# Sample queries times cached keys, and probabilities times cached values: fp32 on quarters of the array in place of split operands on the whole

## The chip, the core and the metric

The kernel runs on one core of a Trainium2 chip. A core has a matmul engine (PE, with its weight loads shown apart as PEld), three engines for elementwise work (DVE, ACT, POOL), a queue engine that issues transfers (SP), and 16 DMA engines. The metric is the device time of one launch in microseconds; less is better. PE's clock can be granted at one of two levels, 1.2 or 2.4 GHz; the profile shows the share of the full clock.

## What is computed

One decoder layer serves 512 prompt tokens and 64 sample tokens (eight sequences of eight) with shared weights, in three sub-layers: a block of token mixers, cross-attention into a memory of 256 tokens, and a squared-ReLU MLP. The change is in the cross-attention of the sample tokens, where each sequence has its own cached keys and values:

```python
def cross_attn(h, mem_k, mem_v, w_xq, w_xo):
    B, L, _ = h.shape
    q = (h @ w_xq).reshape(B, L, XA_HEADS, XA_DH)                 # 4 heads of 256
    s = jnp.einsum('blhd,bmhd->bhlm', q, mem_k) * (XA_DH ** -0.5) # 256 memory tokens
    p = jax.nn.softmax(s, axis=-1)
    o = jnp.einsum('bhlm,bmhd->blhd', p, mem_v).reshape(B, L, D_MODEL)
    return o @ w_xo
```

All inputs are fp32. For the sample that is 8 sequences x (256 keys and 256 values) x 1024 features, 16 MB of cached data that are read once.

## The kernel before

**Products.** The kernel keeps fp32 accuracy with a faster type of PE, fp32r: each operand is split into a rounded part (hi) and the rest (lo), and a product is three matmuls, hi x hi, lo x hi, hi x lo (`mm3`, lines 190 to 192). Splitting takes a cast on ACT (L90) and a subtraction on DVE (L91).

**Halves.** The 576 tokens are worked on in two halves of 288: 256 prompt and 32 sample tokens (four sequences) each. `project` (line 367 on) multiplies a half with a 1024 x 1024 weight matrix, in eight pieces of 512 KB; one piece is 24 matmuls of 288 columns into `psg` ("a block of 24" below). For the second half the last two pieces of the first are still there.

**The stream of pieces.** Weights, cached keys and cached values come as pieces [128, 1024] in one fixed order (`plan`), through four raw buffers (`wraw`). `wnext` hands out the next split piece and sees to it that two are split and up to three more are on their way; `wfetch` issues the transfer on SP, `wsplit` casts and subtracts. A raw buffer is free again once its piece is split. `KV_AFTER` says how many of the 8 key and 8 value pieces of a half are used after each of the eight weight pieces of a projection: those of half 0 among the pieces of w_xq (for half 1 of the tokens), those of half 1 among the pieces of w_xo (for half 0). In the same gaps a stage of the prompt's attention runs (`tick`).

**Sample attention.** `keys(half)` and `values(half)` in `cross` give a step for each piece. A key piece holds, for one sequence, two heads in two parts of 128 features. For it `pad` (lines 1053 to 1061) clears an operand `qx` [128, 4, 128] and copies hi and lo of the eight queries into their own columns, so that all sequences, pairs of heads, and hi and lo add up in one accumulator `pso` [128 rows, 2 x 256]; then eight matmuls of 256 columns run (L1086). After the eighth piece `merge` adds the rows of hi and lo (`ssum`, L1045 and L1046), a softmax follows (L965 to L973), transposes (L1069), and for each value piece again a padded, split operand (`pad_p`, L1093 to L1099) and eight matmuls (L1126). The result is merged and transposed (L1110) and split into the output projection's operand.

**What sets the order.** Each engine runs its instructions in the order that the build gives them; what a wait holds up is all that stands behind it on its engine. Key pieces of a half are called K0 to K7 below and value pieces V0 to V7; a run is a row of such pieces with no other work between.

Of the kernel before, what the change touches and what calls it, by code (L numbers as in the profile page):

```python
# [22 lines left out]
# order of the mixers: (head, retention)  # L23
UNITS = ((0, 1), (0, 0), (1, 0), (1, 1), (2, 0), (2, 1), (3, 0), (3, 1))
# [8 lines left out]
# columns of the packed constants  # L33
# [21 lines left out]
def decoder_step(ctx, tc, xT, memT, ktc, vc, s_gla, s_ret, w_in, w_ga, w_a2, w_mix, w_xq, w_xk, w_xv, w_xo,  # L55
# [24 lines left out]
    # until the first operands arrive: the table of the activations, and the array's clock  # L80
# [58 lines left out]
    # for the second half of the tokens, the last two pieces are still there, and the first few if kept  # L139
    def keep(ts, n):  # L140
        return ts[:2] + [(t, True) for t in ts[2:2 + n]] + ts[2 + n:]
# [9 lines left out]
    def kvtiles(a, half):  # L151
        return [flat(a[half * 4 + b])[:, m * 1024:(m + 1) * 1024] for b in range(4) for m in range(2)]
# [11 lines left out]
    def wfetch():  # L164
        if plan:
            src = plan.pop(0)
            src, stay = src if isinstance(src, tuple) else (src, False)
            raw = wp.tile([P, 1024], F32, name="wraw", bufs=4)
            nc.sync.dma_start(out=raw if len(src.shape) == 2 else raw.rearrange("p (k n) -> p k n", n=src.shape[2]), in_=src)
            raws.append((raw, stay))  # L170
# [23 lines left out]
    def gemm(ps, w, xh, xl, c, k0=0, k1=KT):  # L194
        """ps = w.T @ x for columns c, over k-tiles."""
# [13 lines left out]
    def meansq(ss, n, t, eps=EPS):  # L209
        """mean + eps, tokens on partitions [t, n], from partial sums of squares [128, any, n*t]."""  # L210
# [25 lines left out]
    def bcast(dg, n, t):  # L236
        """the same on all partitions [128, n*t] (PSUM)"""
# [4 lines left out]
    def sumsq(ss, src, first, eng=nc.vector):  # L242
        """ss += src**2, with src [128, 2, n]."""
# [8 lines left out]
    def prenorm(src, half, g, oh, ol, ss):  # L252
        """(oh, ol) = split of rmsnorm(src) on one half of the tokens."""
# [147 lines left out]
    def to(y, g, ss):  # L401
        """y = g * result, ss = partial sums of the result squared"""
# [9 lines left out]
    def residual(y, r, half, ss, ss2=None, g2=None, oh=None, ol=None, scale=None, done=None):  # L412
        """res = r(pair) + norm(y), y with its gain; (oh, ol) = split of g2 * res, ss2 = partial sums of res**2"""
# [22 lines left out]
    kk = biga.tile([P, 2, 2, 1024], F32R, name="kk", tag="biga")        # [d, hi/lo, pair of heads, (h dt m)]  # L436
    vv = kvp.tile([P, 2, 2, 1024], F32R, name="vv")                     # [m, hi/lo, mt, (h d)]
# [808 lines left out]
```

## Time and profile before

| | |
|---|---|
| three runs | 1235.25, 1236.43, 1236.87 us (median 1236.43) |
| span of the profiled execution | 1236.8 us |
| PE busy | 1208.1 us, 98% |
| DVE, ACT, POOL busy | 60%, 46%, 15% |
| DMA | 149.5 MB, 121 GB/s in the mean |
| matmuls for sample keys (L1086) and values (L1126) | 128 each, 256 columns |
| pieces of cached keys and values | 32, 512 KB each |

The profile is of one execution of the program. A row of the timeline gives the start of an instruction and how long it lasted; matmuls are pipelined, so a matmul starts long before the one ahead has ended, and the cost of one is the distance between two starts. "x2" in a row are two records in one row. `a<-b,c` means that tile a is written from b and c; "128\*128" in a matmul's row is the part of the array that it uses, rows by columns, and then come rows and columns of the moving operand.

### The profile page before, as it was taken

How to read it: one execution, taken by the hardware profiler on the slowest of the kernel's cores; microseconds unless marked ns; L12 is line 12 of the kernel's file. 1: busy time of each engine (PE TensorE's matmuls, PEld its weight loads, DVE VectorE, ACT ScalarE, POOL GpSimd, SP SyncE). 2: the span in 40 equal slices, each digit the busy share in tenths (PEclk: the TensorE clock that was granted, in tenths of full speed). 3: DMA queues.
4: the chain of work that ended last, by engine and by line, in shares of the span. 5: the costliest groups of instructions: out<-in, count | busy, mean ns of one | idle time of the engine just before them, and what ended most of it. 6: DMA issues, size and time to landing. Idle time of an engine off the chain costs nothing.

```text
span 1236.8 us, 22417 instructions
## 1 busy us (share of the span) xinstructions
PE 1208.1 (98%) x9202; PEld 1195.9 (97%) x9202; DVE 737.7 (60%) x1287; ACT 567.4 (46%) x1016; POOL 179.3 (15%) x208
## 2 busy tenths in 40 slices
PE   8999999999999999999999999999999999999995
PEld 8999999999999999999999998999999999999995
DVE  6757666666756675668677777793124334323544
ACT  6624555534553455445666667663223213212431
POOL 1521213131312131210013131000000000000000
PEclk9999999999999999999999999999999999999998
DMA  8753324233323242424555566342222222222402
GB/s 269 245 178 100 122 86 124 86 108 100 112 87 122 86 124 86 124 83 139 183 172 166 191 216 212 120 154 68 86 86 86 84 76 80 86 86 86 137 7 71
DMA packets 60374, 149.46 MB, mean 121 GB/s; under 512 B 5520, under 2 KB 30224, under 8 KB 60144
## 3 DMA queue, kind: packets, MB, share of 16 engines
q1 hardware_dynamic: 60272, 148.04, 38.3%
q8 instruction: 72, 1.18, 0.4%
q14 instruction: 30, 0.25, 0.1%
HBM read 134.12 MB, written 13.89 MB: 120 GB/s over the span
## 4 chain that ended last, share of the span: by engine, by line
PE 90%; DVE 3%; ACT 2%; DMA 2%; POOL 1%; issue 1%; POOLq 0%; SPq 0%; DVEq 0%; ACTq 0%
PE psg L190 26%; PE psg L192 26%; PE psg L191 26%; DVE wl L91 1%; PE psa L190 1%; PE psa L192 1%; PE psa L191 1%; ACT wh L90 1%; PE psa L215 1%; DMA wraw<-in_w_xq 1%; PE pso L1086 1%; PE psa L765 1%; PE pso L891 1%; PE pso L892 1%; PE psa L893 1%
## 5 line engine op out<-in xcount | busy, mean ns | idle before, releaser
L190 PE MATMUL psg<-xh,wh 128*128 128x288 f32 x1808 | 536.1, 297 | 1.2 <-DVE y L567 0.6
L191 PE MATMUL psg<-xh,wl 128*128 128x288 f32 x1808 | 532.5, 295 | 1.7 <-DVE wl L91 1.7
L192 PE MATMUL psg<-xl,wh 128*128 128x288 f32 x1808 | 532.5, 295 | 0.0
L190 PEld LDWEIGHTS psg<-xh,wh 128*128 128x128 f32 x1808 | 339.3, 188 | 2.6 <-issue 1.0
L191 PEld LDWEIGHTS psg<-xh,wl 128*128 128x128 f32 x1808 | 339.3, 188 | 2.3 <-DVE wl L91 2.1
L192 PEld LDWEIGHTS psg<-xl,wh 128*128 128x128 f32 x1808 | 338.8, 188 | 1.0 <-DVE xl L91 0.8
L91 DVE TENSOR_TENSOR wl<-wraw,wh 128x1024 fp32r<-128x1024 f32 x221 | 271.4, 1232 | 94.3 <-ACT wh L90 93.5
L90 ACT CAST wh<-wraw 128x1024 fp32r<-128x1024 f32 x221 | 230.7, 1049 | 169.6 <-PE psg L192 130.0
L190 PE MATMUL psg<-bh,wh 128*128 128x288 f32 x640 | 189.4, 296 | 1.1 <-DMA xr<-in_xT 1.1
L192 PE MATMUL psg<-bl,wh 128*128 128x288 f32 x640 | 188.7, 295 | 0.0
L191 PE MATMUL psg<-bh,wl 128*128 128x288 f32 x640 | 188.6, 295 | 0.0
L190 PEld LDWEIGHTS psg<-bh,wh 128*128 128x128 f32 x640 | 120.1, 188 | 1.8 <-ACT wh L90 1.3
L191 PEld LDWEIGHTS psg<-bh,wl 128*128 128x128 f32 x640 | 120.1, 188 | 0.3 <-DVE wl L91 0.2
L192 PEld LDWEIGHTS psg<-bl,wh 128*128 128x128 f32 x640 | 120.0, 188 | 0.2 <-DVE bl L91 0.2
L228 POOL TENSOR_TENSOR rs<-ms,mhalf 96x3 f32<-96x3 f32 (+1 forms) x9 | 8.8, 983 | 522.3 <-DVE ms L227 408.5
L530 DVE TENSOR_TENSOR hr<-hr 128x576 f32<-128x576 f32 x32 | 24.2, 757 | 90.4 <-ACT hr L529 90.4
L529 ACT ACTIVATE hr<-psg 128x576 f32<-128x576 f32 x32 | 20.8, 651 | 106.7 <-PE psg L192 106.7
L549 DVE TENSOR_TENSOR y<-psg,y 128x576 f32<-128x576 f32 x16 | 12.1, 757 | 62.7 <-PE psg L192 62.7
L751 ACT COPY vt<-psg 128x512 f32<-128x512 f32 x16 | 9.4, 586 | 77.8 <-PE psg L192 77.8
L680 POOL TENSOR_TENSOR rs<-mv,mhalf 128x1 f32<-128x1 f32 (+1 forms) x40 | 26.8, 670 | 108.4 <-DVE mv L675 60.7
L753 DVE COPY vd<-psg 128x96 f32<-128x96 f32 x32 | 6.7, 251 | 50.7 <-ACT vt L751 50.7
L869 POOL TENSOR_TENSOR ks<-kx,ks 32x512 fp32r<-32x512 f32 x16 | 22.6, 1411 | 96.8 <-ACT ks L868 85.6
(284 smaller groups left out, 1745.0 us busy)
## 6 DMA issues: line engine op xcount, KB each, us to landing
wraw<-in_w_in SPq DMA_DIRECT2D x64, 512.0 KB, 3.7
wraw<-in_w_up SPq DMA_DIRECT2D x34, 512.0 KB, 3.6
wraw<-in_w_down SPq DMA_DIRECT2D x34, 512.0 KB, 3.6
wraw<-in_ktc SPq DMA_DIRECT2D x16, 512.0 KB, 4.6
wraw<-in_vc SPq DMA_DIRECT2D x16, 512.0 KB, 4.5
wraw<-in_w_xq SPq DMA_DIRECT2D x14, 512.0 KB, 4.0
wraw<-in_w_xo SPq DMA_DIRECT2D x14, 512.0 KB, 4.5
wraw<-in_w_mix SPq DMA_DIRECT2D x12, 512.0 KB, 5.0
```

Of the source, the lines that this page charges most:

```text
L90: nc.scalar.copy(hi, src)
L91: nc.vector.tensor_tensor(out=lo, in0=src, in1=f32(hi), op=ALU.subtract)
L190: nc.tensor.matmul(out, ah, bh, start=first, stop=False)
L191: nc.tensor.matmul(out, al, bh, start=False, stop=False)
L192: nc.tensor.matmul(out, ah, bl, start=False, stop=last)
L215: nc.tensor.matmul(ps[:t, i:i + 1], ss[:, l, i * t:(i + 1) * t], ones[:, 0:1], start=l == 0, stop=l == ls - 1)
L529: nc.scalar.activation(r, ps, AF.Relu)
L530: nc.vector.tensor_tensor(out=r, in0=r, in1=r, op=ALU.mult)
L680: nc.gpsimd.tensor_tensor(out=rs[:t], in0=mv[:t], in1=mhalf[:t, 0:1], op=ALU.pow)
L765: nc.tensor.matmul(sc[:, :P], kf[:, ci], qf[:, ci], start=True, stop=True)
L869: nc.gpsimd.tensor_tensor(out=ks[32:64], in0=kx[32:64], in1=f32(ks[32:64]), op=ALU.subtract)
L891: nc.tensor.matmul(so[:, :256], lq, s0h[:, j], start=False, stop=False)
```

## The change

- Cached keys and values are no longer split. `wsplit` passes a raw piece on as it is (mode RAW), and its products read the raw buffer. It is free again when these have run. The four raw buffers stay four; a raw piece that waits to be used counts among the three that may be on their way.
- The operands of the sample are fp32 and made once per half: `operand()` clears [128, 8, 4, 32], four sums of hi and lo put the queries in. For the values, four copies out of the transposed probabilities do the same.
- Four matmuls per piece in place of eight, one for each head: 32 columns of the stationary operand (four sequences of eight), on the head's own 32 columns of the array (`tile_position=(0, 32 * h)`), and so into 32 rows of the accumulator. The cached keys are laid out so that a piece holds all four heads of one part.
- With a row for each head and token there is nothing to merge: the softmax runs on [128, 1, 256] straight from the accumulator, and there are two transposes of 128 x 128 where there were four of 64 x 64.
- `KV_AFTER` spreads the pieces as 2, 3, 3, 0, 3, 3, 2, 0 over the weight pieces, before 4, 4, 0, 3, 3, 2, 0, 0.

```diff
-KV_AFTER = (((0, 4), (4, 8), (8, 8), (8, 11), (11, 14), (14, 16), (16, 16), (16, 16)),
-            ((0, 4), (4, 8), (8, 8), (8, 11), (11, 14), (14, 16), (16, 16), (16, 16)))
+KV_AFTER = (((0, 2), (2, 5), (5, 8), (8, 8), (8, 11), (11, 14), (14, 16), (16, 16)),) * 2
...
     def kvtiles(a, half):
-        return [flat(a[half * 4 + b])[:, m * 1024:(m + 1) * 1024] for b in range(4) for m in range(2)]
+        return [(flat(a[half * 4 + b])[:, m * 1024:(m + 1) * 1024], RAW) for b in range(4) for m in range(2)]
...
     def wsplit():
         if raws:
-            raw, stay = raws.pop(0)
-            pool = staying[-1] if stay else wp
+            raw, mode = raws.pop(0)
+            if mode == RAW:
+                ready.append((raw,))
+                return
+            pool = staying[-1] if mode == STAY else wp
...
     def wnext(n=P):
-        while len(ready) < 2 and (raws or plan):
-            while len(raws) < 3 and plan:
+        while sum(len(r) == 2 for r in ready) < 2 and (raws or plan):
+            while plan and len(raws) + sum(len(r) == 1 for r in ready) < N_RAW - 1:
                 wfetch()
+            if not raws:
+                break
             wsplit()
...
+    def operand():
+        x = x1.tile([P, KT, 4, 32], F32, name="qx")
+        nc.gpsimd.memset(x, 0.0)
+        return x
+
+    def quarters(acc, x, w, first, last):
+        for h in range(HEADS):
+            rows = slice(32 * h, 32 * h + 32)
+            nc.tensor.matmul(acc[rows, :256], x(h), w[:, h], start=first, stop=last, skip_group_check=True,
+                             tile_position=(0, 32 * h))
...
     def keys(half):
         c0 = half * NH + 256
         s = Env({"i": 0, "acc": None})
-
-        def pad(b, m):
...
+        qx = operand()
+        for b in range(4):
             qc = slice(c0 + b * 8, c0 + b * 8 + 8)
...
+            nc.gpsimd.tensor_tensor(out=qx[:, :, b, b * 8:b * 8 + 8], in0=f32(qh[:, :, qc]), in1=f32(ql[:, :, qc]), op=ALU.add)
...
         def step():
...
-            for n in range(4):
-                out = s.acc[:, (n // 2) * 256:(n // 2 + 1) * 256]
-                for kx in w:
-                    nc.tensor.matmul(out, q[:, n, :], kx[:, n], start=s.i == 1 and n == 0 and kx is w[0],
-                                     stop=s.i == 8 and n == 3 and kx is w[1], skip_group_check=True)
+            w, = wnext(256)
+            quarters(s.acc, lambda h: qx[:, 2 * h + dt, b], w, s.i == 1, s.i == 8)
             if s.i == 8:
-                pend[half] = softmax(merge(s.acc), 64, "psm", rsx[half][:64, 2:3])
+                pend[half] = softmax(s.acc[:, :256].rearrange("p (j m) -> p j m", j=1), P, "psm", rsx[half][:, 2:3])
                 e.side.append(turn())
```

How the instructions stand, at three places. First PE, where K0 of the first half ends, before (`pso` is the accumulator, `wh` and `wl` the split piece, `psg` the projection, `kk` the prompt's keys, `bh` and `bl` its queries; the numbers tell buffers apart):

```order
L1086 MATMUL pso_8447<-wh_8384,qx_8448 128x256
L1086 MATMUL pso_8447<-wl_8385,qx_8448 128x256
L190 MATMUL psa_8488<-kk_7494,bh_8090 128x256
L191 MATMUL psa_8488<-kk_7494,bl_8091 128x256
L1086 MATMUL pso_8447<-wh_8454,qx_8458 128x256
L192 MATMUL psa_8488<-kk_7494,bh_8090 128x256
L190 MATMUL psa_8488<-kk_7494,bh_8090 128x256
L191 MATMUL psa_8488<-kk_7494,bl_8091 128x256
```

PE at the start of the same piece after (x4 are the four heads of one piece; `wraw` is the raw piece):

```order
L199 MATMUL psg_8424<-xh_7489,wl_8310 128x288
L200 MATMUL psg_8424<-xl_7490,wh_8309 128x288
L1056 MATMUL pso_8449<-wraw_8307,qx_8418 32x256 x4
L1056 MATMUL pso_8449<-wraw_8341,qx_8418 32x256 x4
L198 MATMUL psa_8460<-kk_7494,bh_8090 128x256
L199 MATMUL psa_8460<-kk_7494,bl_8091 128x256
L200 MATMUL psa_8460<-kk_7494,bh_8090 128x256
L198 MATMUL psa_8460<-kk_7494,bh_8090 128x256
```

The eight matmuls of a piece, hi and lo in turn on the whole array, became four on 32 columns each; K0 and K1 stand as one run, and the prompt's products are no longer mixed into them. In each half the quarters stand in nine runs: K0 K1, K2 K3, K4, K5 K6, K7, V0 V1, V2, V3 V4 V5, V6 V7.

Second DVE, from the last key product of the first half to the scaled probabilities `psm`, before (in brackets what an instruction waits for; `xl` belongs to the prompt's attention, `p` and `smx` to both softmaxes):

```order
L1046 TENSOR_TENSOR ssum<-pso,ssum 32x512 [waits Activation_49]
L965 TENSOR_REDUCE mx<-ssum 64x2 [waits DVE_49]
L965 TENSOR_REDUCE mx<-psa 128x2 [waits PE_49]
L966 TENSOR_SCALAR mx<-mx,rsx_82 64x2 [waits DVE_49]
L966 TENSOR_SCALAR mx<-mx,rsx_82 128x2 [waits DVE_49]
L91 TENSOR_TENSOR xl<-psa,xh 128x2x256 [waits Activation_49]
L91 TENSOR_TENSOR wl<-wraw,wh 128x1024 [waits DMAHW4_49]
L971 RECIPROCAL smx<-smx 64x2 [waits Activation_49]
L973 TENSOR_SCALAR psm<-psm,smx 64x256 [waits DVE_49]
L973 TENSOR_SCALAR psm<-psm,smx 64x256
```

The same stretch of DVE after:

```order
L93 TENSOR_TENSOR wl<-wraw,wh 128x1024 [waits DMAHW2_49,Activation_49]
L973 TENSOR_REDUCE mx<-pso 128x1 [waits PE_49]
L93 TENSOR_TENSOR xl<-psa,xh 128x2x256 [waits Activation_49]
L974 TENSOR_SCALAR mx<-mx,rsx_82 128x1 [waits DVE_49]
L93 TENSOR_TENSOR wl<-wraw,wh 128x1024 [waits DMAHW3_49,Activation_49]
L980 RECIPROCAL smx<-smx 128x1 [waits Activation_49]
L93 TENSOR_TENSOR xl<-psa,xh 128x2x256 [waits Activation_49]
L982 TENSOR_SCALAR psm<-psm,smx 128x256 [waits DVE_49]
```

The second merge and half the columns are gone, the maximum comes from the accumulator, and between it and `psm` stand two `xl` and one `wl`.

Third SP, eight transfers from V3 of the first half on, before (DVE is the split that frees the buffer):

```order
L169 DMA wraw_8853<-in_vc 128x1024 [waits DMAHW3_49,DVE_49,Activation_49]
L169 DMA wraw_8897<-in_vc 128x1024 [waits DMAHW4_49,DVE_49,Activation_49]
L169 DMA wraw_8925<-in_vc 128x1024 [waits DMAHW5_49,DVE_49]
L169 DMA wraw_8955<-in_w_xq 128x1024 [waits DMAHW6_49,DVE_49,Activation_49]
L169 DMA wraw_8975<-in_vc 128x1024 [waits DMAHW7_49,DVE_49,Activation_49]
L169 DMA wraw_9010<-in_vc 128x1024 [waits DMAHW0_49,DVE_49]
L169 DMA wraw_9045<-in_w_xq 128x1024 [waits DMAHW1_49,DVE_49]
L169 DMA wraw_9077<-in_w_xq 128x1024 [waits DMAHW2_49,DVE_49,Activation_49]
```

SP from V3 on after (PE is the product that frees the buffer):

```order
L172 DMA wraw_8800<-in_vc 128x1024 [waits DMAHW4_49,PE_49]
L172 DMA wraw_8821<-in_vc 128x1024 [waits DMAHW7_49,DVE_49]
L172 DMA wraw_8842<-in_vc 128x1024 [waits DMAHW5_49,PE_49]
L172 DMA wraw_8874<-in_w_xq 128x1024 [waits DMAHW6_49,PE_49]
L172 DMA wraw_8880<-in_vc 128x1024 [waits DMAHW0_49,PE_49]
L172 DMA wraw_8886<-in_vc 128x1024 [waits DMAHW1_49,PE_49]
L172 DMA wraw_8893<-in_w_xq 128x1024 [waits DMAHW2_49,PE_49]
L172 DMA wraw_8923<-in_w_xo 128x1024 [waits DMAHW3_49,DVE_49]
```

Of these eight issues six wait for a product where all waited for a split. Each buffer is the one that was released first, so the last weight piece of the half takes over V5's.

## Rows read from the trace of the kernel before

**Rows 1.** the page: span, PE, chain, two groups (busy us, mean ns | idle)
```profile
span 1236.8 us, 22417 instructions
PE 1208.1 (98%) x9202; PEld 1195.9 (97%) x9202; DVE 737.7 (60%) x1287; ACT 567.4 (46%) x1016; POOL 179.3 (15%) x208
...
PE 90%; DVE 3%; ACT 2%; DMA 2%; POOL 1%; issue 1%; POOLq 0%; SPq 0%; DVEq 0%; ACTq 0%
...
L91 DVE TENSOR_TENSOR wl<-wraw,wh 128x1024 fp32r<-128x1024 f32 x221 | 271.4, 1232 | 94.3 <-ACT wh L90 93.5
L90 ACT CAST wh<-wraw 128x1024 fp32r<-128x1024 f32 x221 | 230.7, 1049 | 169.6 <-PE psg L192 130.0
```

**Rows 2.** PE, stretch of the change: us, busy (records), clock, DMA, GB/s
```profile
661.20:777.70 116.50, 109.75 (x834) 0.99 0.63 200
```

**Rows 3.** timeline of PE, one sample-key piece (start us, us, engine, operation)
```profile
661.18 0.27 PE L1086 MATMUL pso<-wh,qx 128*128 128x256 f32 x1
...
662.12 0.28 PE L190 MATMUL psa<-kk,bh 128*128 128x256 f32 x1
```

**Rows 4.** timeline of PE, an fp32 product and an fp32 transpose
```profile
103.70 0.38 PE L765 MATMUL psa<-qf,kf 128*128 128x128 f32 x2
103.92 0.27 PE L766 MATMUL psa<-idn,kf 128*128 128x128 f32 x1
```

**Rows 5.** timeline of PE, one-column products, and 64-row transposes between matmuls
```profile
654.67 0.95 PE L215 MATMUL psa<-idn,ss 128*128 128x1 f32 x8
655.48 0.38 PE L190 MATMUL psg<-xh,wh 128*128 128x288 f32 x1
...
776.46 0.29 PE L191 MATMUL psg<-xh,wl 128*128 128x288 f32 x1
776.68 0.46 PE L1110 MATMUL psa<-idn,ssum 64*128 64x64 f32 x4
...
777.31 0.30 PE L190 MATMUL psg<-xh,wh 128*128 128x288 f32 x1
```

**Rows 6.** timeline of PE at the probabilities' transposes, both halves [idle, releaser]
```profile
687.07 0.29 PE L192 MATMUL psg<-xl,wh 128*128 128x288 f32 x1
689.49 0.31 PE L1069 MATMUL psa<-idn,psm 64*128 64x64 f32 x2 [2.12 <-ACT p L970]
...
749.65 0.29 PE L192 MATMUL psg<-xl,wh 128*128 128x288 f32 x1
750.85 0.30 PE L1069 MATMUL psa<-idn,psm 64*128 64x64 f32 x2 [0.90 <-DVE psm L973]
```

**Rows 7.** timeline of DVE in the chain ahead of the first of these
```profile
684.78 0.69 DVE L1046 TENSOR_TENSOR ssum<-pso,ssum 32x512 f32<-32x512 f32 x1
685.50 0.68 DVE L965 TENSOR_REDUCE mx<-ssum 64x2 f32<-64x512 f32 x1
...
688.99 0.61 DVE L973 TENSOR_SCALAR psm<-psm,smx 64x256 f32<-64x256 f32 x2
```

**Rows 8.** waits of weight loads and PE, 661 to 777: total, times, longest
```profile
PEld psg L191 <- DVE wl L91: 2.1, 2, 1.1
PEld pso L1086 <- POOL qx L1060: 1.3, 4, 0.5
PEld pso L1126 <- DVE qx L91: 1.1, 3, 0.7
...
PEld psg L190 <- ACT wh L90: 0.9, 2, 0.7
...
PE psa L1110 <- DVE ssum L1046: 0.4, 1, 0.4
```

**Rows 9.** PE after the first of these waits (columns as in rows 2)
```profile
689.80:711.50 21.70, 21.70 (x158) 0.92 0.62 199
```

**Rows 10.** raw pieces' transfers; GB/s in 40 slices of 661 to 777
```profile
DMA to landing us min/median/max: 3.4/3.9/8.8
...
GB/s 3 174 333 222 116 191 331 259 171 34 174 181 0 264 281 210 227 280 199 273 244 48 196 307 323 199 55 281 261 167 102 242 121 96 263 267 233 331 171 175
```

More of the change, by code (lines that the diff above doesn't have):

```diff
@@ L22 @@
 N_WARM = 20
+N_RAW = 4
 UNITS = ((0, 1), (0, 0), (1, 0), (1, 1), (2, 0), (2, 1), (3, 0), (3, 1))
 KEEP_MIX, KEEP_FFN = 2, 4
[L27 to L28 removed]
+RING, STAY, RAW = 0, 1, 2
+KV_AFTER = (((0, 2), (2, 5), (5, 8), (8, 8), (8, 11), (11, 14), (14, 16), (16, 16)),) * 2
 V_PRE_MIX, V_POST_MIX, V_PRE_XA, V_POST_XA, V_PRE_FFN, V_POST_FFN, V_MEM, V_GLA, V_RET, V_B = (
@@ L140, in keep @@
     def keep(ts, n):
-        return ts[:2] + [(t, True) for t in ts[2:2 + n]] + ts[2 + n:]
+        return ts[:2] + [(t, STAY) for t in ts[2:2 + n]] + ts[2 + n:]
     def rest(ts, n):
@@ L441, in memkv @@
             for m in range(2):
-                raw = wp.tile([P, 1024], F32, name="wraw", bufs=4)
+                raw = wp.tile([P, 1024], F32, name="wraw", bufs=N_RAW)
                 nc.sync.dma_start(out=raw, in_=flat(src)[:, m * 1024:(m + 1) * 1024])
@@ L962, in softmax @@
     def softmax(s, t, name, r):
-        mx = x2.tile([P, 2], F32, name="mx")
+        mx = x2.tile([P, 2], F32, name="mx")[:, :s.shape[1]]
         nc.vector.reduce_max(mx[:t], s, axis=AX.X)
         nc.vector.tensor_scalar(out=mx[:t], in0=mx[:t], scalar1=r, scalar2=-1.0, op0=ALU.mult, op1=ALU.mult)
-        sm = x2.tile([P, 2], F32, name="smx")
-        p = x2.tile([P, 2, 256], F32, name=name, bufs=2 if t == P else 1)
-        for i in range(2):
+        sm = x2.tile([P, 2], F32, name="smx")[:, :s.shape[1]]
+        n = s.shape[1]
+        p = x2.tile([P, n, 256], F32, name=name, bufs=n)
+        for i in range(n):
             nc.scalar.activation(p[:t, i], s[:, i], AF.Exp, bias=mx[:t, i:i + 1], scale=r, accum_out=sm[:t, i:i + 1])
         nc.vector.reciprocal(sm[:t], sm[:t])
-        for i in range(2):
+        for i in range(n):
             nc.vector.tensor_scalar(out=p[:t, i], in0=p[:t, i], scalar1=sm[:t, i:i + 1], scalar2=None, op0=ALU.mult)
@@ L1035, in cross @@
     pend = {}
-    def pads(n):
-        return slice((n // 4) * 64, (n // 4) * 64 + 32), slice((n // 4) * 64 + 32, (n // 4) * 64 + 64)
-    def merge(x):
-        s = x1.tile([64, 2, 256], F32, name="ssum")
-        sf = s.rearrange("p a m -> p (a m)")
-        for n in range(2):
-            nn = slice(n * 32, n * 32 + 32)
-            nc.scalar.copy(sf[nn], x[n * 64 + 32:n * 64 + 64, :])
-            nc.vector.tensor_tensor(out=sf[nn], in0=x[n * 64:n * 64 + 32, :], in1=sf[nn], op=ALU.add)
-        return s
+    def operand():
[7 more added lines that the diff above has]
+                             tile_position=(0, 32 * h))
     def keys(half):
@@ L1066, in turn @@
             pt = atile()
-            for j in range(2):
-                for mm in range(2):
-                    nc.tensor.transpose(pt[:, (2 * j + mm) * 64:(2 * j + mm + 1) * 64], p[:64, j, mm * P:(mm + 1) * P], ident[:64, :64])
-            ptf = x1.tile([P, 4, 64], F32, name="ptf")
-            nc.scalar.copy(ptf.rearrange("p n t -> p (n t)"), pt[:, :256])
-            pend[half] = ptf, pad_p(ptf, 0, 0)
+            for mt in range(2):
+                nc.tensor.transpose(pt[:, mt * P:(mt + 1) * P], p[:, 0, mt * P:(mt + 1) * P], ident)
+            px = operand()
+            pend[half] = px
+            ptv = pt[:, :256].rearrange("p (n b t) -> p n b t", b=4, t=8)
+            for b in range(4):
+                eng = nc.scalar.copy if b % 2 else nc.vector.tensor_copy
+                eng(px[:, :, b, b * 8:b * 8 + 8], ptv[:, :, b])
         def step():
-            b, m = s.i // 2, s.i % 2
+            b, dt = s.i // 2, s.i % 2
             s.i += 1
@@ L1104, in values, with turn @@
         s = Env({"i": 0, "acc": None})
-        def turn(o):
+        def turn(acc):
+            o = x1.tile([P, 256], F32, name="osum")
+            nc.scalar.copy(o, acc[:, :256])
             yield
             pt = atile()
-            for j in range(4):
-                nc.tensor.transpose(pt[:, j * 64:(j + 1) * 64], o.rearrange("p a m -> p (a m)")[:, j * P:(j + 1) * P], ident[:64, :64])
-            for n in range(2):
-                split(ah[:, 4 * n:4 * n + 4, c0:c0 + 32], al[:, 4 * n:4 * n + 4, c0:c0 + 32],
-                      pt[:, :256].rearrange("p (j t) -> p j t", t=64)[:, :, n * 32:n * 32 + 32])
+            for dt in range(2):
+                nc.tensor.transpose(pt[:, dt * P:(dt + 1) * P], o[:, dt * P:(dt + 1) * P], ident)
+            for dt in range(2):
+                split(ah[:, dt::2, c0:c0 + 32], al[:, dt::2, c0:c0 + 32],
+                      pt[:, dt * P:(dt + 1) * P].rearrange("p (h t) -> p h t", t=32))
         def step():
+            b, mt = s.i // 2, s.i % 2
             s.i += 1
@@ L1118, in step @@
                 s.acc = otile()
-                s.ptf, s.p = pend[half]
-            px, w = s.p, wnext(256)
-            if s.i < 8:
-                s.p = pad_p(s.ptf, s.i // 2, s.i % 2)
-            for h in range(4):
-                out = s.acc[:, (h % 2) * 256:(h % 2 + 1) * 256]
-                for vx in w:
-                    nc.tensor.matmul(out, px[:, h, :], vx[:, h], start=s.i == 1 and h == 0 and vx is w[0],
-                                     stop=s.i == 8 and h == 3 and vx is w[1], skip_group_check=True)
+            w, = wnext(256)
+            quarters(s.acc, lambda h: pend[half][:, mt * HEADS + h, b], w, s.i == 1, s.i == 8)
             if s.i == 8:
-                e.side.append(turn(merge(s.acc)))
+                e.side.append(turn(s.acc))
         return step
```

30 lines of the change are left out of this document (6 added, 24 removed).

## The prediction

> **What bounds the kernel now.** I read the page first. PE is busy 98% of a span of 1236.8 us, and the chain that ended last runs over PE for 90% of it [rows 1]. So what counts is how far PE's starts lie apart, and where it stands still. The durations printed for matmuls overlap and are of no use for this. Next comes the stretch that the change touches, from the first sample-key product at 661.2 us to the end of the first half of the output projection at 777.7 us: PE is busy 109.75 of 116.5 us there [rows 2]. Some 7 us of standing still can be won besides PE's own work, and what a lowered clock costs. Then I read the waits of that stretch [rows 6, 8], who made them long [rows 7], the clock [rows 9] and the transfers that feed it [rows 10].
>
> **Multiplications.** Before, a 512 KB piece costs eight fp32r matmuls of 256 columns; they start at 661.18 and the next work at 662.12 [rows 3]: 0.94 us a piece, 30.1 us for 32 pieces. After, a piece costs four fp32 matmuls on 32 columns of the array each. An fp32 matmul is two records in the trace: L765, one call in the code, stands as x2 and takes from 103.70 to 103.92, so 0.11 us a record with 128 columns [rows 4] and 0.22 us with 256. No row of the trace has matmuls on separate groups of columns. So the bounds are: all four quarters side by side, 2 x 0.22 = 0.44 us a piece, 14.1 us in all (-16.0); none side by side, 8 x 0.22 = 1.76 us, 56.3 us (+26.2). I choose by the order of the records. The two of one quarter write the same columns, so the second must follow the first; and the rows show PE starting matmuls in the order of the code [rows 3, 4]. If it keeps that order, and lets a matmul run beside the one before only where the columns differ, then the second record of a quarter runs beside the first of the next, and nothing more does: each quarter adds one record's time. That is 4 x 0.22 = 0.88 us a piece, 28.2 us in all, **-1.9 us**. The packing then pays for the doubled passes and for little else.
>
> The Trainium skill speaks of this in "TensorE: Matmul & The Clock Gate" (Part 3: Packing small matmuls): matmuls on separate tiles overlap, a pack taking one matmul's duration and about 4 ns a tile, and matmuls start and end strictly in program order. The first rule alone would make a piece 0.44 us, both together 0.88 us; no row here shows either.
>
> **Loading the stationary operand.** Eight matmuls of one column each follow one another in 0.81 us, 654.67 to 655.48, which is their weight loads alone: 0.10 us for 128 columns [rows 5], about 0.025 for 32. If a quarter's load can begin only once the record before it has started, 128 x 0.025 = 3.2 us come on top; hidden, as those of [rows 3] are, they cost nothing. Neither end is nearer, so I take the middle, **+1.6 us**.
>
> **Changing the shape of the array.** The nearest row is a run of transposes that use 64 rows of the array (64\*128): from L191 at 776.46 to L190 at 777.31 are 0.85 us [rows 5], in which two matmuls of 288 columns (0.13 each, by the 0.94 / 8 of [rows 3]) and four transposes of 64 columns (0.055 each, by [rows 4]) need 0.48. So going to another shape and back costs 0.37 us. The quarters stand in nine runs per half, 18 in all: +6.7 us. The six runs of 64-row transposes (two for the probabilities and one for the output in each half) become full 128 x 128 ones: -2.2 us, and their own time stays about 1 us. Sum **+4.5 us**; if groups of columns cost no such change, -2.2.
>
> **Waits that go.** In both halves PE stands before the transposes of the sample's probabilities: 687.07 to 689.49 and 749.65 to 750.85, less a matmul's 0.13, are 2.3 + 1.1 = 3.4 us [rows 6]. It waits there for a chain on DVE and ACT: merging rows of hi and lo (a copy on ACT, 0.69 on DVE), maxima over 512 columns (0.68), exponentials, and two scalings (0.61) [rows 7]. After, nothing is merged and there are half as many columns. From the last key product to those transposes PE has 12 products, four transposes, 24 products and two transposes: 1.4 + 0.4 + 3.2 + 0.2 = 5.2 us. Against that stand half of 0.68 and of 0.61, one exponential where two were (under 0.8), and ahead of them on DVE three subtractions that the order shows (one wl of 1.23 [rows 1], two xl of half its columns): some 4 us. So the wait goes. Next late would be the copies into the padded operand, and they have a block of 24 products before them. The weight loads' waits for padded hi and lo operands (1.3 + 1.1) go as well, since the operands are now made once per half; of these 2.4 us some would be hidden anyway, and I take 1.6, and 0.4 for the merged output [rows 8]. After the 2.3 us of standing still the granted clock averages 0.92 over 21.7 us, so part of that ran at 1.2 instead of 2.4 GHz [rows 9]: 1.7 us of work lost, which should not come again without the wait. Sum **-7.1 us**; the ends are 0 (all replaced by others) and -7.9.
>
> **The ring of raw pieces.** Before, every transfer waits for a split on DVE. After, most transfers of keys and values wait for products on PE, and the four raw buffers are all the prefetch there is; on SP all later pieces, weights included, queue behind a late one. The place to look at is the last weight piece of each half. Its buffer is freed by V5, the last of a run of three value pieces. After V5 PE still has 24 products, V6 and V7 with a change of shape, and one product that needs no wl: 3.2 + 1.8 + 0.4 + 0.1 = 5.5 us. The transfer takes 3.4 us at the least; two issued just before it share the engines, whose best slice moved 333 GB/s, 1.6 us a piece, so it lands 3.8 to 5.1 us after V5 [rows 10]. Cast and subtraction are 1.05 + 1.23 [rows 1]. That makes 6.1 to 7.4 us, a wait of 0.6 to 1.9 in each half, in the middle 1.3, so 2.6 us. Before, weight loads waited 2.1 + 0.9 us for splits [rows 8]. So **-0.4 us**, between -1.8 and +0.8.
>
> **At nothing.** 32 casts and 32 subtractions leave ACT and DVE; apart from the waits above PE did not wait for them. POOL clears twice the columns at a time and makes four sums of hi and lo per half. Between the last value product and the next half's first key product stand two blocks of 24, 6.3 us, and that hides it; what goes beyond 6.3 would be paid once. The new order of the cached keys is made outside the kernel.
>
> **Sum.** -1.9 + 1.6 + 4.5 - 7.1 - 0.4 = **-3.3 us**. The profiled execution's span, 1236.8, lies inside the three runs (1235.25 to 1236.87) with nothing around it, so the sum goes against their median: 1236.43 - 3.3 = **1233.1 us**. With loads, operands' waits and ring at their lower ends it is -7.1, 1229; with loads and ring at their upper ends and the wait for the probabilities staying, it is +2.9, 1239.
>
> **Rivals.** *All quarters run side by side* (A). For it: four separate groups of columns, and only the order of the records against it. Against it: [rows 4] shows the two records of a call next to each other. The pieces cost 14.1 us. PE then outruns the ring: the same count with 0.44 us leaves 4.6 us where 6.1 to 7.4 are needed, 2.1 a half, and the weight piece before it comes late too, by about 1.3; 6.8 us against 3.0. -16.0 + 4.5 - 7.1 + 3.8 = -14.8, so **1222**. It is the Trainium skill's rule on packs (the section above) taken alone.
>
> *Nothing overlaps* (C), the slower side. Place: the 128 quarter products. Price: 1.76 us a piece. For it: every start in [rows 3, 4] comes when the one before has had time for all its columns. Against it: there all matmuls use the same columns. The ring keeps up then, and its waits go: +26.2 + 4.5 - 7.1 - 3.0 = +20.6, so **1257**. It decides from about 1.0 us a piece: without exposed loads the sum is zero at 0.88 + 4.9 / 32 = 1.03 us.
>
> *The ring starves PE* (D): quarters as in my forecast, but the last two weight pieces of a half come 1.5 us later than counted, since one transfer has taken up to 8.8 us [rows 10]. -3.3 + 4 x 1.5 = +2.7, so **1239**, between 1236 and 1242.
>
> **How the numbers follow.** Forecast 0.47, A 0.20, C 0.20, D 0.13. About 0.2%, 2.5 us, is what a measurement of this kernel can tell from no change. Faster: A and 0.6 of the forecast, 0.48. Same: 0.34 of the forecast and 0.4 of D, 0.21. Slower: C, the rest of D and a little of the forecast, 0.31. The range is 1220 to 1257: it cuts off the better part of A's spread and the worse part of C's, less than 0.2 together. The forecast's own range is 1229 to 1239.
>
> **What would show it.** Per quarter, the sample products' starts should be 0.22 us apart for the forecast, 0.11 for A, 0.44 for C, and a run of them should cost some 0.4 us at its two edges. There should be no idle time before the probabilities' transposes, a granted clock of 1.00 throughout, and a wait for wl of about 1.3 us before the last weight piece of each half. I am wrong if a piece takes clearly over 1 us, if PE waits for transfers before the key or value products themselves, or if the clock falls again.

## Result, and the profile after

The changed kernel takes 1224.28 us in the median of four runs (1221.84 to 1225.24), against 1236.65 for the kernel before, run beside it: a ratio of 0.9897, 95% interval 0.9885 to 0.9908, or 12.4 us less. The profiled execution has a span of 1222.0 us. The direction and the range of the prediction (1220 to 1257) held; the time is nearest to that of rival A (1222); the forecast (1233.1) was 9 us above it.

The page after, in the order of [rows 1] (span; busy time, share and instructions of the engines; the chain; two groups with busy us, mean ns and idle):

```profile
span 1222.0 us, 22137 instructions
...
PE 1193.4 (98%) x9194; PEld 1170.8 (96%) x9194; DVE 692.9 (57%) x1217; ACT 527.9 (43%) x944; POOL 155.2 (13%) x156
...
PE 93%; DMA 2%; ACT 2%; DVE 2%; issue 1%; POOL 0%; SPq 0%; POOLq 0%; DVEq 0%; ACTq 0%
...
L93 DVE TENSOR_TENSOR wl<-wraw,wh 128x1024 fp32r<-128x1024 f32 x189 | 233.2, 1236 | 105.2 <-ACT wh L92 104.3
L92 ACT CAST wh<-wraw 128x1024 fp32r<-128x1024 f32 x189 | 197.9, 1050 | 173.2 <-PE psg L200 122.8
```

PE is still the bound. DVE and ACT have 45 and 40 us less to do: 32 casts and 32 subtractions are gone (x221 was, x189 is), and the merging with them. The stretch of the change, as in [rows 2] (us, PE's busy time and records, granted clock, DMA share, GB/s), from the first sample-key product to the end of the first half of the output projection:

```profile
660.80:766.10 105.30, 98.00 (x850) 0.98 0.68 228
```

It was 116.5 us and is 105.3. PE stood still 6.75 us of it before and stands still 7.3 now, so all of the gain is in PE's own work, and the waits did not shrink.

**A piece.** Timeline of PE at the first two key pieces, from four windows of it, to be held against [rows 3]; a row counts the records that run in the window and gives the first start among them:

```profile
660.59 0.29 PE L200 MATMUL psg<-xl,wh 128*128 128x288 f32 x1
660.81 0.42 PE L1056 MATMUL pso<-wraw,qx 128*32 128x256 f32 x4
...
661.05 0.61 PE L1056 MATMUL pso<-wraw,qx 128*32 128x256 f32 x8
...
661.26 0.61 PE L1056 MATMUL pso<-wraw,qx 128*32 128x256 f32 x8
...
661.81 0.39 PE L198 MATMUL psa<-kk,bh 128*128 128x256 f32 x1
662.03 0.28 PE L199 MATMUL psa<-kk,bl 128*128 128x256 f32 x1
```

Four records start at once at 660.81 (7 ns apart in the trace's own times), four more at 661.05, four at 661.26, and what follows the two pieces starts at 661.81. A piece is two rounds of four records, 0.43 to 0.46 us, where it was 0.94. A quarter's two records, called its two passes below, are 0.22 us apart, which is what [rows 4] give for 256 columns; but all four quarters make their first pass together and then all four their second.

**Waits.** What PE itself waited for in 655 to 780 us (total, times, longest), after:

```profile
PE psg L198 <- ACT wh L92: 3.1, 3, 1.8
PE psg L199 <- DVE wl L93: 2.6, 4, 0.9
PE psa L198 <- DVE ptl L93: 1.4, 1, 1.4
```

and before, the same two kinds (those at the probabilities' transposes and the operands are [rows 6, 8]):

```profile
PE psg L191 <- DVE wl L91: 1.7, 2, 0.9
...
PE psg L190 <- ACT wh L90: 0.5, 1, 0.5
```

The wait at the probabilities' transposes and those for padded operands are gone, as forecast. In their place PE waits for split weight pieces: 5.7 us against 2.2, and once 1.4 us for `ptl` of the prompt's attention. The timeline shows where (in brackets the idle time before the row, and what ended it):

```profile
696.98 0.29 PE L200 MATMUL psg<-xl,wh 128*128 128x288 f32 x1
697.21 1.59 PE L1056 MATMUL pso<-wraw,qx 128*32 128x256 f32 x24
700.56 0.40 PE L198 MATMUL psg<-xh,wh 128*128 128x288 f32 x1 [1.76 <-ACT wh L92]
701.82 0.40 PE L199 MATMUL psg<-xh,wl 128*128 128x288 f32 x1 [0.86 <-DVE wl L93]
...
704.85 0.29 PE L200 MATMUL psg<-xl,wh 128*128 128x288 f32 x1
705.07 1.07 PE L1056 MATMUL pso<-wraw,qx 128*32 128x256 f32 x16
...
707.45 0.40 PE L199 MATMUL psg<-xh,wl 128*128 128x288 f32 x1 [0.37 <-DVE wl L93]
...
754.34 0.40 PE L198 MATMUL psg<-xh,wh 128*128 128x288 f32 x1 [1.08 <-ACT wh L92]
755.60 0.61 PE L199 MATMUL psg<-xh,wl 128*128 128x288 f32 x1 [0.86 <-DVE wl L93]
...
760.07 0.29 PE L200 MATMUL psg<-xl,wh 128*128 128x288 f32 x1
```

Each long wait stands right behind a run of value pieces: three of them (x24) and then 1.76 + 0.86 us until a weight piece's hi and lo are there; two (x16), and 0.37 more; and in the second half again. The block of 24 that follows takes 3.03 us in the first half (701.82 to 704.85) but 4.47 in the second (755.60 to 760.07), because there the granted clock fell to about half (1.2 of 2.4 GHz):

```profile
757.00:759.00 2.00, 2.00 (x10) 0.53 0.90 326
```

### The profile page after: what moved, and what is told of

It reads as the page before. It is cut to its first block, busy times and chain, and to the rows that moved or that the text cites. A ratio compares the mean times of both kernels' runs of the same rounds, so it can differ in the third digit from the quotient of the medians.

```text
span 1222.0 us, 22137 instructions
## 1 busy us (share of the span) xinstructions
PE 1193.4 (98%) x9194; PEld 1170.8 (96%) x9194; DVE 692.9 (57%) x1217; ACT 527.9 (43%) x944; POOL 155.2 (13%) x156
## 4 chain that ended last, share of the span: by engine, by line
PE 93%; DMA 2%; ACT 2%; DVE 2%; issue 1%; POOL 0%; SPq 0%; POOLq 0%; DVEq 0%; ACTq 0%
PE psg L198 27%; PE psg L200 27%; PE psg L199 27%; PE psa L198 2%; PE psa L200 1%; PE psa L199 1%; PE pso L1056 1%; DMA wraw<-in_w_xo 1%; PE psa L223 1%; ACT wh L92 1%; PE psa L773 1%; PE pso L899 1%; PE pso L900 1%; PE psa L901 1%; PE psa L776 1%; PE psa L833 1%
## 5 line engine op out<-in xcount | busy, mean ns | idle before, releaser
L93 DVE TENSOR_TENSOR wl<-wraw,wh 128x1024 fp32r<-128x1024 f32 x189 | 233.2, 1236 | 105.2 <-ACT wh L92 104.3
L92 ACT CAST wh<-wraw 128x1024 fp32r<-128x1024 f32 x189 | 197.9, 1050 | 173.2 <-PE psg L200 122.8
L258 DVE TENSOR_TENSOR ss<-ss,sq 128x576 f32<-128x576 f32 x34 | 26.3, 773 | 16.8 <-ACT sq L257 16.7
```

The costliest lines, as they stand in the source:

```text
L92: nc.scalar.copy(hi, src)
L93: nc.vector.tensor_tensor(out=lo, in0=src, in1=f32(hi), op=ALU.subtract)
L258: eng.tensor_tensor(out=ss, in0=ss, in1=sq[:, :, :n], op=ALU.add)
```

## The experiments

All kernels but k2 are the changed one with a single edit; kr5 and k4 have the places of before and one edit more. "Place 0" to "place 7" are the gaps after the eight weight pieces of a half, where key and value pieces and side work (a stage of the prompt's attention per `tick`) stand. Ratios are to the kernel before, run on the same chip. Runs without an interval are single executions; they are there for their traces, and their times are good for large differences only.

### Do the quarters keep the order of the program?

My forecast let one record of a quarter overlap one of the next, since PE starts matmuls in the order of the code. Two runs cut each quarter product in two halves of 128 columns, in opposite orders.

```diff
-        for h in range(HEADS):
-            rows = slice(32 * h, 32 * h + 32)
-            nc.tensor.matmul(acc[rows, :256], x(h), w[:, h], start=first, stop=last, skip_group_check=True,
+        for h, c in [(h, c) for h in range(HEADS) for c in range(2)]:
+            rows, cols = slice(32 * h, 32 * h + 32), slice(128 * c, 128 * c + 128)
+            nc.tensor.matmul(acc[rows, cols], x(h), w[:, h, cols], start=first, stop=last, skip_group_check=True,
```

That is e1. In e2 only the loop's first line differs:

```diff
+        for h, c in [(h, c) for c in range(2) for h in range(HEADS)]:
```

> Each quarter product is cut into two of 128 columns, and the two of one head stand next to each other (h0 left, h0 right, h1 left, ...); the arithmetic is the same. In order: a product waits until the columns of the array that it needs are free, and everything behind it in the program waits too. Then the right half of a head runs only beside the left half of the next, a piece takes 4 x 0.22 = 0.88 us and not 0.44, the time is 1224.3 + 32 x 0.44 = 1238 us, and starts within a piece are 0.22 us apart in pairs. Own streams: each quarter of the columns works through its own products, whatever the program order between quarters. Then a piece stays at 0.44 us and the time at 1222 to 1226 us.

> The same eight products of 128 columns per piece as in the run with the halves of a head next to each other, in the other order: the left halves of all four heads, then the right halves. In order: no product meets its own columns within four, so 0.44 us a piece, 1222 to 1226 us. Own streams: the same. If cutting the products itself costs something (twice the weight loads), it shows here: 8 more starts of 7 ns are 0.06 us a piece, 1226 us at most.

In both, part of the sample's sums is lost, probably because the first piece starts a head's sums a second time with its right half; all products run, and the time can be read. Timeline of PE in e1 over the first two pieces (the first row from a window that ends with the first of them):

```profile
661.37 0.66 PE L1056 MATMUL pso<-wraw,qx 128*32 128x128 f32 x16
...
661.37 1.12 PE L1056 MATMUL pso<-wraw,qx 128*32 128x128 f32 x32
662.42 0.38 PE L198 MATMUL psa<-kk,bh 128*128 128x256 f32 x1
```

Sixteen records of 0.11 us start in the first 0.43 us of e1, and two pieces take 1.05 us with what comes at the end, in e2 1.01, where the uncut quarters take 1.00. In e1 the right half of head 0 stands ahead of the left half of head 1 in the program and uses the columns that head 0's left half has not yet left. If everything behind it had waited, as I had assumed, the two pieces would have taken 1.8 us. So each group of columns works through its own products, and a group that has to wait does not hold the others. The whole executions took 1228.5 and 1228.1 us, some 4 us more than the changed kernel and above the range expected for own streams. The surplus is nearly the same in both orders, so the order of the halves does not cause it; PE's waits from 655 to 800 us add up to 9.3 and 8.6 us, against 7.1 in the changed kernel. Whether cutting the products causes that was not followed up.

### What is the packing worth?

In e3 every product uses all 128 columns (the call in `values` is changed as the one in `keys` shown here).

```diff
-            rows = slice(32 * h, 32 * h + 32)
-            nc.tensor.matmul(acc[rows, :256], x(h), w[:, h], start=first, stop=last, skip_group_check=True,
-                             tile_position=(0, 32 * h))
+            nc.tensor.matmul(acc[:, :256], x(h).rearrange("p b t -> p (b t)"), w[:, h], start=first and h == 0,
+                             stop=last and h == HEADS - 1, skip_group_check=True)
...
-            quarters(s.acc, lambda h: qx[:, 2 * h + dt, b], w, s.i == 1, s.i == 8)
+            quarters(s.acc, lambda h: qx[:, 2 * h + dt], w, s.i == 1, s.i == 8)
```

> The sample products stay unsplit in fp32, but each uses all 128 columns of the array: the operands of all four sequences against each piece, and all heads summed into the same rows. That leaves out the separation of heads and sequences, so only the time is of use. The packing pays: a piece is 4 x 2 x 0.22 = 1.76 us and not 0.44, the changes of shape go (18 runs x 0.3 us), and the waits for weight pieces (some 6 us) go since the ring has time: 1224.3 + 42.2 - 5.4 - 6 = 1255 us. The gain came from the lost splits and waits and the packing is nearly worthless: under 1235 us.

1251.44 us, 15.6 more than the kernel before beside it (1235.84). Timeline of PE, the two pieces K2 and K3 of the first half:

```profile
669.34 0.29 PE L200 MATMUL psg<-xl,wh 128*128 128x288 f32 x1
669.48 3.62 PE L1055 MATMUL pso<-wraw,qx 128*128 128x256 f32 x16
672.93 0.60 PE L1007 MATMUL psa<-idn,p 128*128 128x128 f32 x4
```

Sixteen records take from 669.48 to 672.93, 0.216 us each, 1.73 a piece. Waits for weight pieces are gone; PE stands still 0.9 and 0.8 us ahead of V0 of the two halves instead, for what the trace does not show. So fp32 products without the packing are a loss: nearly twice the PE time of the split ones, and more than the lost splits and waits give back. The whole gain comes from four quarters in the time of one. The rows also settle the edges: from the last matmul (669.34) to the first record is 0.14, as between any two matmuls, and a run of fp32 products on the whole array costs nothing at its edges (the first of the 18 runs is an exception, with 0.19 more ahead of it). With quarters it does: 660.59 to 662.03 above is 1.44 us, where two pieces and two ordinary steps make 0.87 + 0.25, so 0.32 a run.

### Where the pieces stand

```diff
-KV_AFTER = (((0, 2), (2, 5), (5, 8), (8, 8), (8, 11), (11, 14), (14, 16), (16, 16)),) * 2
+KV_AFTER = (((0, 4), (4, 8), (8, 8), (8, 11), (11, 14), (14, 16), (16, 16), (16, 16)),) * 2
```

> The changed kernel with the places of the keys and values of before: 4 and 4 key pieces after the first two weight pieces, then 3, 3 and 2 value pieces. The ring of four raw pieces is what PE waits for: four pieces in a row take 4 x 0.44 = 1.8 us and a transfer takes 1.6 us at the best rate, so the run of keys waits for its own transfers, some 2 x 1.6 us twice a half; 1228 to 1234 us, with waits for wraw before the sample products. The spreading is of no account: 1222 to 1226 us.

It fell out the other way: 1217.4 us in a single execution. Timed:

> The changed kernel with the places of the keys and values of before, timed: the single look gave 1217.4 us, 6.9 under the changed kernel's median. The new places are what starves the ring: 1216 to 1219 us. The look was one lucky execution: 1222 to 1226 us.

1220.21 us, ratio 0.9859 (0.9844 to 0.9874): the new places cost some 0.4%, 4 to 5 us of what the quarters bring. Neither bound of the expectation was met to the us, but the two intervals (0.9885 to 0.9908 for the change) do not touch. PE's waits in 655 to 780 us:

```profile
PE psg L199 <- DVE wl L93: 1.7, 3, 0.9
PE pso L1056 <- DMA wraw<-in_vc: 0.6, 1, 0.6
...
```

With two short ones (0.4 and 0.2) that is 2.9 us, against 7.1 in the change.

The same places put into the kernel before, nothing else changed:

> The kernel before with the places of keys and values of the changed kernel, and nothing else of the change. There every raw piece is freed by a split and not by PE, and a piece takes 0.94 us of PE, so transfers are not short: no change, ratio 0.998 to 1.002. If the new places are bad in themselves (the last values two weight pieces later), it is slower here too, by some 4 us, ratio 1.003.

1240.80 us, ratio 1.0041 (1.0025 to 1.0057): slower there too, by as much. PE's waits for weight pieces were 2.2 us and are, over 655 to 810 us, since the stage now ends later:

```profile
PE psg L189 <- ACT wh L89: 2.4, 2, 1.7
...
PE psg L190 <- DVE wl L90: 2.1, 3, 0.9
```

All of PE's waits there add up to 9.1 us, against 6.4 before. So the change is two changes: quarters, worth some -1.4%, and new places, +0.4%, whichever way the products are done. In k2 every buffer is freed by a split and not by PE, so what follows explains the change and not k2, where the reason stays open.

### Why the new places cost

Three explanations were tried (the first two edits are shortened). In w1 weight pieces no longer queue behind the last raw piece on SP:

```diff
-            plan += ([t] if t is not None else []) + kv[after[0]:after[1]]
+            if t is not None:
+                plan.insert(len(plan) - (min(ahead, 1)), t)
+            plan += kv[after[0]:after[1]]
+            ahead = after[1] - after[0]
...
-        return [a.rearrange("p (k n) -> p k n", n=n) for a in ready.pop(0)]
+        return [a.rearrange("p (k n) -> p k n", n=n) for a in (pieces if kv else ready).pop(0)]
```

In r5 there is a fifth buffer for keys and values; to make room for it, the merged output takes the buffer of the probabilities:

```diff
-            raw = wp.tile([P, 1024], F32, name="wraw", bufs=N_RAW)
+            since[0] += 1
+            if mode == RAW and extra and since[0] > N_RAW:
+                raw = extra[0].tile([P, 1024], F32, name="kraw")
+                since[0] = 0
+            else:
+                raw = wp.tile([P, 1024], F32, name="wraw", bufs=N_RAW)
...
-            while plan and len(raws) + sum(len(r) == 1 for r in ready) < N_RAW - 1:
+            while plan and len(raws) + sum(len(r) == 1 for r in ready) < N_RAW - 1 + len(extra):
```

> The changed kernel with its new places, but each weight piece is fetched and split one piece earlier, ahead of the last key or value piece before it; buffers and products are the same. Weight pieces are late because they queue behind pieces of keys and values whose buffers only PE frees: the waits for wh and wl (3.1 + 2.6 us) shrink to under 2, 1218 to 1221 us. The ring lacks throughput altogether: the waits move to the sample products (for wraw), and the time stays at 1222 to 1226 us.

> The changed kernel with its new places and a fifth raw buffer for keys and values during the stage (the merged output takes the place of the probabilities to make room). Four buffers are too few: one more transfer is under way at any time, the waits for wh and wl (5.7 us) shrink to under 2, 1217 to 1221 us. The transfers themselves are the limit, shared among more of them each takes longer: 1222 to 1226 us.

Neither helped, and both times lie in the second range of their expectation: w1 1223.46 us, ratio 0.9889 (0.9874 to 0.9903); r5 1223.77, 0.9889 (0.9869 to 0.9909). PE's waits in w1, where part of the wait moved to the value pieces themselves:

```profile
PE pso L1062 <- DMA wraw<-in_vc: 2.8, 3, 1.1
PE psg L204 <- ACT wh L92: 2.3, 2, 2.1
PE psg L205 <- DVE wl L93: 0.6, 3, 0.3
```

and in r5:

```profile
PE psg L204 <- ACT wh L92: 4.1, 2, 2.3
PE psg L205 <- DVE wl L93: 2.1, 4, 0.7
```

In k3 fewer pieces stand in one place:

```diff
-KV_AFTER = (((0, 2), (2, 5), (5, 8), (8, 8), (8, 11), (11, 14), (14, 16), (16, 16)),) * 2
+KV_AFTER = (((0, 4), (4, 8), (8, 8), (8, 10), (10, 12), (12, 14), (14, 16), (16, 16)),) * 2
```

> The changed kernel with the keys at the places of before (4, 4, 0) and the values two at a time over four weight pieces, so that they end as late as in the change. Three value pieces and a weight piece in one place are more than the transfers bring (4 x 1.26 us in some 5 us of products): with 2 and 1 the waits for wh and wl fall under 1 us, 1216 to 1218 us. What counts is that two weight pieces without values follow the last value, before the next half's keys: it is as slow as the change, 1222 to 1225 us.

k3 was the worst, above both cases of its expectation: 1229.61 us, 0.9946 (0.9931 to 0.9962), with waits for weight pieces of

```profile
PE psg L198 <- ACT wh L92: 7.2, 5, 2.9
PE psg L199 <- DVE wl L93: 3.7, 5, 0.9
```

Taken with the traces of the others this tells what they have in common. The work of PE in the places 3 to 7 of the first half, in matmuls (w the projection, q quarters in pieces, s side work), read off the traces:

```
place      3                     4                       5        6        7
changed    24w 6s              | 24w 2q 12s 1q 12s     | 24w 3q | 24w 2q | 24w
k1         24w 2q 16s 1q 4s    | 24w 2q 12s 1q 12s     | 24w 2q | 24w    | 24w
k3         24w 2q 20s          | 24w 2q 24s            | 24w 2q | 24w 2q | 24w
```

The side work runs out after nine calls of `tick`, in all three at the end of place 4. The values after that have only 24 products (3.2 us) between them: five value pieces in the change, four in k3, two in k1. And PE stands still there: in the change after the 3q (700.56) and the 2q (707.45), in k3 after both 2q, up to 2.9 us (and once behind its eight keys). k1 waits least. How it comes about is in the transfers of the change. SP's issues (start, us, tile, count):

```profile
689.88 2.41 SPq L172 DMA_DIRECT2D wraw<-in_vc  x3
692.51 0.33 SPq L172 DMA_DIRECT2D wraw<-in_w_xq  x1
697.90 0.80 SPq L172 DMA_DIRECT2D wraw<-in_vc  x2
698.86 0.33 SPq L172 DMA_DIRECT2D wraw<-in_w_xq  x1
```

the rate from 689.5 to 706 us in 40 slices, and the time from issue to landing of the pieces issued in 683 to 706:

```profile
GB/s 0 0 40 149 99 328 407 258 129 139 119 189 248 377 417 407 427 427 387 278 179 99 60 60 298 328 318 397 407 437 328 407 417 338 328 397 278 179 79 50
...
DMA to landing us min/median/max: 3.7/5.1/6.9
```

V3 can only be issued once PE has used V0 (689.88), V4 once weight piece 5 is split (690.94), V5 behind it into the buffer of V1 (691.91), and weight piece 6 once PE has used V2 (692.51). Two silent slices ahead show that nothing was under way until then: the four buffers held weight piece 5 and V0, V1 and V2, which PE used only from 689.18 on. V3 lands at 693.6, and V4 only 3.2 us later, though it was issued 1.1 us behind (why was not followed up). Then V5 and weight piece 6 come at some 410 GB/s, 1.27 us a piece, but the latter lands 6.9 us after its issue, at 699.4, and cast and subtraction (1.05 + 1.24 us by the page after) take until 701.7. PE had 12 side products, 24 projection products and three pieces for that time, and was through at 698.8.

The last run tests it with the change's own places and buffers: side work is held back for the last values.

```diff
-                        if n == n0 + 1:
+                        if n == n0 + 1 and i > 1:
                             tick()
```

> The changed kernel with its new places of keys and values and four buffers; the only edit is that the attention of the prompt's tokens (the side work) is advanced once, not twice, at each of the first four weight pieces of a half, so that some of it is left for the last five values. In the traces so far PE stands still right behind values that have no side work beside them, and nowhere else for long. If that is the cause, the side work covers the transfers: 18 more products (2.4 us) before the weight piece after the values of place 5, 12 (1.6 us) after those of place 6; the 7 us of PE's waits there fall to 2 or less, the clock does not fall, and the time is 1216 to 1219 us, ratio to before 0.984 to 0.987. If the last values simply end too late, whatever stands beside them, nothing changes: 1223 to 1225 us, ratio 0.989 to 0.991.

1218.00 us, ratio 0.9852 (0.9827 to 0.9876): the 0.4% that the new places cost is back, with the new places. PE's waits in 655 to 780 us:

```profile
PE psg L198 <- ACT wh L92: 1.8, 2, 1.5
PE pso L1056 <- DMA wraw<-in_ktc: 1.7, 2, 1.2
PE psg L199 <- DVE wl L93: 0.2, 1, 0.2
```

Waits are 3.7 us in place of 7.1, and the clock averages 1.00 over the stage. Those for weight pieces fell from 5.7 to 2.0 us, and the 1.4 for `ptl` went too. Nearly half of what is left are new ones, for keys, in the first places, from which the side work was taken. So the last values do not end too late. They end when there is nothing left for PE to do beside their transfers.

### Two more variants

> The places of before and the fifth buffer together. What waits are left with the places of before (1.7 us for wl, 0.4 for the probabilities) come from the ring: 1215 to 1216 us. They come from DVE and ACT: the same as with the places of before alone, 1217 us.

The places of before with the fifth buffer: 1216.12 us, ratio 0.9829 (0.9814 to 0.9844), the fastest of all, 21 us under the kernel before and 8 under the change. Here the fifth buffer helps by some 0.3% (the two intervals just touch). Which wait it takes is not plain from the traces, as 1.7 us for `wl` stay.

> The changed kernel with the places of before and no side work between the pieces of one place: the quarters stand in about 10 runs in all, not 18. A run of quarters costs 0.30 us at its edges: 8 x 0.3 = 2.4 us less than the 1220.2 of that kernel with side work between, so 1217 to 1218 us. The side work that is now late (attention of the prompt's tokens) is waited for at the end of each half, or four pieces in a row wait for their transfers: 1220 us or more.

```diff
-                        if n == n0 + 1:
-                            tick()
```

k4 (with the places of before) saves edges but took 1223.39 us, ratio 0.9893 (0.9874 to 0.9911), 3 us more than k1. It fits that pieces in a row outrun their transfers, or that side work comes late, as the second case of the expectation says; the only trace kept of k4 is of an execution of 6610 us, in which PE was busy nearly throughout, and it shows none of these waits, so that stays open.

## Why the prediction was right in direction and 9 us off

The range held because it was drawn wide enough to take in most of A and C. The forecast's own range, 1229 to 1239, did not hold, and of the three signs of being wrong one came: the clock fell again. The direction was right by the waits that go (-7.1), with a price for the products that was far too high.

- **Multiplications, -1.9 us forecast, -16.0 measured.** This is the step that failed, 32 x (0.44 - 0.94) us, and it is more than the whole error. Of the two bounds, 0.44 and 1.76 us a piece, I chose 0.88 "by the order of the records". The two records of a product next to each other in [rows 4] came from one product alone on the array; they show that its second pass follows its first, not that the second pass of one holds up the first pass of another. The trace after shows that it does not, and e1 that the order of the program between the quarters does not matter either. The rows could not decide between A and the forecast, and a chance of 0.20 for A was too little. The Trainium skill's "TensorE: Matmul & The Clock Gate" (Part 3: Packing small matmuls) gives a pack one matmul's duration and about 4 ns a tile; the traces agree with the first and show 7 ns. The same section of the Trainium skill has matmuls start strictly in program order; by that rule two pieces of e1's cut products would take an estimated 1.76 us, and 1.05 was measured.
- **Loads, +1.6 forecast, 0 measured.** Quarters that start 7 ns apart leave no room for a load of 0.025 us each.
- **Shape changes, +4.5 forecast, +3.6 measured.** 18 runs cost 0.32 us at their edges, not 0.37, 5.8 us; the full transposes that replaced the 64-row ones cost nothing at theirs. In this timeline of PE six transposes of 0.109 us (four of the prompt's and the two of the sample's) and two steps of 0.13 make 0.92 of the 0.93 us from 685.10 to 686.03:

```profile
685.10 0.30 PE L200 MATMUL psg<-xl,wh 128*128 128x288 f32 x1
685.24 0.60 PE L1007 MATMUL psa<-idn,p 128*128 128x128 f32 x4
685.67 0.38 PE L1072 MATMUL psa<-idn,psm 128*128 128x128 f32 x2
...
686.03 0.30 PE L199 MATMUL psg<-xh,wl 128*128 128x288 f32 x1
```

  e3 excludes that the type of the operands is what costs. The Trainium skill's "TensorEngine Tiling (Array Packing)" (Tiling Modes) says that a change of tiling mode drains the engine; the 0.32 us at the edges agree with that.
- **Waits that go, -7.1.** They went, all of them. The clock did fall once more, after another wait: 4.47 - 3.03 = +1.4 us.
- **Ring, -0.4 forecast, +4.9 measured** (3.5 for weight pieces, 1.4 for `ptl`). I had looked at the last weight piece of a half, and with pieces of 0.88 us. With 0.44 it is the piece before it that comes late, by 1.76 + 0.86 us in the first half, and the last one by 0.37. Rival A's working had the size (+3.8 in place of -0.4) and named both pieces, but put 2.1 at the last and 1.3 at the one before it. What I did not see is that the new places were a change of their own, to be costed apart: I counted products between a piece's release and its use, but not that the side work ends before the values do.
- **Sum as measured:** -16.0 + 0 + 3.6 - 7.1 + 1.4 + 4.9 = -13.2 us; the medians differ by 12.4, the two profiled spans by 14.8.

Rival A's sum (-14.8) had the right mechanism and nearly the right size. Rivals C and D did not occur, though D's mechanism, weight pieces late behind raw ones, took back 3.5 us of the 16.0 that the products gained.

## What to carry to other kernels

When products are packed on separate columns of the array, count the pack as one of its products with all its passes (here four equal ones), and look for the bill at the edges of a run and in what now runs out of cover. A piece that is read raw by PE holds its buffer until PE has used it, so each piece placed behind it starts its transfer later; spread such pieces so that other work of PE lies beside the last of them, and test a change of places apart from the change that it comes with.

## What was not expected of the hardware

- The two passes of fp32 products on four groups of columns run interleaved, four first passes and then four second ones, with starts 7 ns apart; with the halves of a head in a row (e1) it is nearly the same time, 1.05 us for two pieces against 1.00.
- A run of products on 32 columns costs 0.32 us at its edges, fp32 products on the whole array between fp32r ones 0.
- Queued transfers of 512 KB arrive 1.27 us apart from the second of a row on, at some 410 GB/s; I had taken 1.6 from the best slice of [rows 10], which were 2.9 us long.
- The granted clock fell to about half (1.2 GHz) behind such a wait in the second half of the change (1.08 + 0.86 us, above), but not behind the longer one in its first half (1.76 + 0.86). It fell in k3 too, behind its keys, where PE's row for 676 to 680 us reads

```profile
676.00:680.00 4.00, 3.16 (x13) 0.51 0.50 169
```

  What sets the difference was not tested.
